# Second modulation in the attention phase: products on GpSimd, sums on ScalarE one unit later, in place of one VectorE instruction

## The chip, the cores and the metric

The kernel runs on one core of a Trainium2 chip. The metric is the device time of one execution in microseconds (us), taken as the median of several runs. The profile is of one execution. Its engines are PE (TensorE: matmuls, with PEld for its weight loads), DVE (VectorE), ACT (ScalarE), POOL (GpSimd) and SP (SyncE, which here only issues DMAs). ACT and POOL issue DMAs as well.

## The reference

One layer of a diffusion backbone: a modulation, differential attention with a residual and a layer norm, a second modulation, and an expert feed-forward with a second residual and layer norm. All data are float32; there are 512 latent tokens, 256 context tokens and a width of 1024.

```python
mod = (s_c @ ada_w[i] + ada_b[i])[:, None, :]          # s_c = silu(c), 1 x 1024; ada_w is 1024 x 6144
sh1, sc1, g1, sh2, sc2, g2 = jnp.split(mod, 6, axis=-1)
u = h * (1.0 + sc1) + sh1
o, oc = diff_attention(uc, u, da_w_in[slot], da_w_out[slot], ...)
h = layer_norm(DN_ALPHA * h + g1 * o, ln_g[i, 0], ln_b[i, 0])
f = peer_ffn(h * (1.0 + sc2) + sh2, peer_wq[i], peer_keys[i], peer_u[i], peer_v[i])
h = layer_norm(DN_ALPHA * h + g2 * f, ln_g[i, 1], ln_b[i, 1])
```

The attention has 8 heads, each with two score maps: `a = softmax(q1 k1) - lam * softmax(q2 k2)`, then `a @ v`, an RMS norm for each head and the output projection. This case is about `g1`, `sh2` and `sc2`: 3 x 1024 numbers, each a dot product of `silu(c)` with one column of `ada_w`.

## The kernel before

The kernel has three phases: attention, mix (rest of the output projection, layer norm, second modulation) and the expert stage (`peer`). Matmuls that need float32 accuracy are made of three matmuls: an operand is split into a rounded high part and a low part, and `mm3` (lines 150, 152 and 153) sums high x high, high x low and low x high. A split is an ACT copy (high, line 142) and a DVE subtraction (low, line 143); `hi_lo` is the helper. Where a helper pins the order, the line is 100.

The modulation that attention itself needs (`sh1`, `sc1`) is computed at the very start with matmuls. The second one, 24 blocks of 128 outputs, runs beside the attention of the heads. Block n is loaded as a tile `adw` with 128 outputs on the partitions and 1024 inputs along the row (512 KB; two buffers). One instruction multiplies it with `sbc`, which is silu(c) repeated on all partitions, and sums each row into column n of `modc`. The function is `ada_units`; each block is a unit. After the last one, `gate` adds the bias, spreads `g1` over a row by transposes on PE, and prepares the columns that mix uses.

For a head, q, k and v are projected (`qkv` banks in PSUM), q and k are rotated (ACT copies `sw`, line 404; DVE products and sums, lines 405, 406 and 424 or 449), split into `kh` (line 142 or 450 on ACT, 143 or 451 on DVE) and sent by DMA from SP into stacked tiles `ks` (line 440) and `qs` (line 456). `kh` has one buffer. Scores (line 523) go to one PSUM tile `sc`; DVE takes row maxima (line 530), ACT the exponentials with row sums (line 534), DVE combines the two maps (line 544, `e`), PE transposes (line 552, `ta`), ACT and DVE split the transposed tile (`at`), and PE multiplies with `vt`. The next score tile can be written only when the exponentials of the one before are done. Weights of the projections come as `wraw` tiles by DMAs from the queue of ACT (line 208), and are split into `whi` and `wlo`.

Three streams of units are merged by due times, which are written by hand in heads: the projections, the attention of the heads, and the second modulation (from 0.55 to 7.9 heads). What is written in that order then goes through a scheduler. It orders each engine's instructions by its own estimate of when each can start, so the order on every engine of the attention phase depends on every unit in it. An instruction on an engine starts in that fixed order; one that has to wait holds back all that stand behind it on the engine, its DMA issues too. The orders of mix and the expert stage are pinned, or come out the same in both kernels.

Of the kernel before, what the change touches and what calls it, by code (L numbers as in the profile page):

```python
# [15 lines left out]
AF = mybir.ActivationFunctionType  # L16
OP = mybir.AluOpType
# [88 lines left out]
class Net:  # L106
# [75 lines left out]
    def attention(self):  # L182
        nc, a, tc = self.nc, self.a, self.tc
        self.dram = self.es.enter_context(tc.tile_pool(name="dram", bufs=1, space=bass.MemoryType.DRAM))
        self.sd = self.dram.tile([1, D], F32, name="sd")
        op = self.onpool = tc.alloc_tile_pool(name="on", bufs=1, side="right")

        one = lambda x: op.tile([128, T], x, name="osc", bufs=H + 1)
# [34 lines left out]
        with tc.tile_pool(name="st", bufs=1) as st, tc.tile_pool(name="stp", bufs=1, space=PSUM) as sp:  # L223
# [20 lines left out]
            AW, MP, HL = {}, {}, {}  # L244
# [113 lines left out]
        sbc = ap.tile([128, D], F32, name="sbc")  # L358
# [261 lines left out]
            return [(h + 1 + lag - (LAST if h == 7 else 0) + 0.25 * x, (0, e, p, 1)) for x, e, p in sorted(out, key=lambda u: u[0])]  # L620

        def ada_units(n0, n1):
            def one(n):
                def go():
                    for k in (n, n + 1):
                        if k < n1 and k not in AW:
                            AW[k] = ap.tile([128, D], F32, name="adw", bufs=2)
                            nc.scalar.dma_start(AW[k], a["ada_b2"][k])
                    ins = nc.vector.scalar_tensor_tensor(AW[n], AW[n], 1.0, sbc, op0=OP.mult, op1=OP.mult,
                                                         accum_out=self.modc[:, n:n + 1])  # L630
                    if self.mark:
                        self.behind(ins, self.mark)
                return (1000, None, go)
            return [one(n) for n in range(n0, n1)]

        AW, self.WH, Z = {}, {}, {}
        self.mark = None
# [67 lines left out]
        for h in range(H):  # L705
            if h < 6:
                A += timed(qkv_units(h), h)
            B += attn_units(h)
        G += timed(ada_units(0, 24), ADA_FROM, GATES_AT - ADA_FROM)
        G.append((GATES_AT, (0, gate, None)))  # L710
        A += timed(qkv_units(6) + qkv_units(7), 6, 1.5)
# [757 lines left out]
```

## Time and profile before

| | us |
|---|---|
| median of 3 runs | 1654.32 |
| the three runs | 1653.97, 1654.32, 1658.24 |
| the profiled execution, its own time | 1652.39 |
| its span (first to last instruction) | 1650.5 |

The profile's idle time names what ended the wait ("<-DMA qs<-kh": the load of `qs` landed last). "PEclk" is the granted clock of TensorE as a share of full speed. Matmuls are pipelined: their durations overlap, so the starts tell the rate.

### The profile page before, as it was taken

The numbers are of one execution on the slowest core, as the hardware profiler recorded it, in microseconds if no ns is written. First come the engines' busy times: TensorE is split into PE (matmuls) and PEld (weight loads), VectorE is DVE, ScalarE is ACT, GpSimd is POOL, SyncE is SP. The second block draws the span as 40 slices with busy tenths as digits, with TensorE's granted clock in tenths as the row PEclk, the third lists the DMA queues.
The fourth block names the chain that finished last, engine by engine and source line by source line (L and its number), as shares of the span: only waits on it lengthen the run. The fifth ranks groups of instructions, "written<-read, shape, count | busy, mean of one in ns | idle before, by whom it ended". The sixth has DMA issues, their size and how long they took to land.

```text
span 1650.5 us, 24717 instructions
## 1 busy us (share of the span) xinstructions
PE 1602.9 (97%) x9229; PEld 1435.6 (87%) x9229; DVE 1422.3 (86%) x2515; ACT 771.8 (47%) x1161; POOL 637.6 (39%) x367
## 2 busy tenths in 40 slices
PE   8899999998999999999999999999999999999997
PEld 5789898986889999999999997888888888888885
DVE  6688888797799999989999848998998989999887
ACT  7565666554433344565566643332333333333332
POOL 0000000000176676535533316665656656655421
PEclk9999999999999999999999999999999999999998
DMA  8644546513432566898899999999999999999982
GB/s 334 182 142 122 156 121 162 168 52 131 156 140 100 159 207 196 283 339 276 301 339 351 347 380 365 358 375 370 386 386 385 388 378 391 390 370 347 341 298 86
DMA packets 134346, 443.80 MB, mean 269 GB/s; under 512 B 13137, under 2 KB 39249, under 8 KB 122962
## 3 DMA queue, kind: packets, MB, share of 16 engines
q1 hardware_dynamic: 79506, 210.88, 37.3%
q0 software_dynamic: 37440, 136.33, 22.1%
q10 hardware_dynamic: 17280, 95.01, 15.6%
q8 instruction: 72, 1.18, 0.3%
q14 instruction: 48, 0.39, 0.1%
HBM read 376.76 MB, written 50.73 MB: 259 GB/s over the span
## 4 chain that ended last, share of the span: by engine, by line
PE 77%; DVE 7%; DMA 6%; issue 5%; POOL 2%; ACT 2%; SPq 0%; ACTq 0%; DVEq 0%; POOLq 0%
PE a L150 10%; PE a L153 10%; PE a L152 10%; PE v L153 9%; PE v L150 9%; PE v L152 9%; PE v L100 4%; PE qkv L150 3%; PE qkv L152 3%; PE qkv L153 3%; PE sc L523 3%; DMA gr<-in_peer_u_dram,eidx 2%; POOL gr L1230 1%; POOL ulo L1154 1%; DMA qs<-kh 1%
## 5 line engine op out<-in xcount | busy, mean ns | idle before, releaser
L150 PE MATMUL a<-u2h,uhi 128*128 128x384 f32 x1024 | 345.5, 337 | 0.2 <-ACT at L100 0.2
L153 PE MATMUL a<-u2h,ulo 128*128 128x384 f32 x1024 | 343.6, 336 | 1.4 <-POOL ulo L1154 1.4
L152 PE MATMUL a<-u2l,uhi 128*128 128x384 f32 x1024 | 343.0, 335 | 0.0
L153 PE MATMUL v<-vh,wl 128*128 128x512 f32 x768 | 300.5, 391 | 3.8 <-DVE wl L143 3.8
L150 PE MATMUL v<-vh,wh 128*128 128x512 f32 x768 | 299.6, 390 | 2.9 <-ACT wh L142 1.5
L152 PE MATMUL v<-vl,wh 128*128 128x512 f32 x768 | 300.1, 391 | 0.1
L1230 POOL DMA_INDIRECT gr<-in_peer_u_dram,eidx x128 | 189.7, 1482 | 245.8 <-DVE gr L1239 230.5
L1154 POOL TENSOR_TENSOR ulo<-ur,uhi 128x1024 fp32r<-128x1024 f32 x77 | 207.4, 2699 | 100.6 <-ACT uhi L100 74.2
L1230 POOL DMA_INDIRECT gr<-in_peer_v_dram,eidx x128 | 180.2, 1408 | 147.1 <-DVE facc L1246 132.3
L142 ACT ACTIVATE vh<-vr 128x1024 fp32r<-128x1024 f32 x126 | 132.7, 1055 | 210.8 <-PE v L153 83.7
L100 POOL TENSOR_TENSOR qlo<-qraw,qhi 128x1024 fp32r<-128x1024 f32 x12 | 28.8, 2399 | 457.6 <-DVE val L100 435.5
L150 PEld LDWEIGHTS a<-u2h,uhi 128*128 128x128 f32 x1024 | 192.8, 188 | 1.8 <-ACT at L100 0.5
L153 PEld LDWEIGHTS a<-u2h,ulo 128*128 128x128 f32 x1024 | 192.6, 188 | 1.8 <-POOL ulo L1154 1.7
L152 PEld LDWEIGHTS a<-u2l,uhi 128*128 128x128 f32 x1024 | 192.9, 188 | 1.3
L143 DVE TENSOR_TENSOR vl<-vr,vh 128x1024 fp32r<-128x1024 f32 x126 | 158.7, 1260 | 30.5 <-ACT vh L142 30.3
L153 PEld LDWEIGHTS v<-vh,wl 128*128 128x128 f32 x768 | 144.5, 188 | 35.7 <-DVE wl L143 5.5
L150 PEld LDWEIGHTS v<-vh,wh 128*128 128x128 f32 x768 | 144.6, 188 | 33.2 <-ACT wh L142 2.2
L1246 DVE SCALAR_TENSOR_TENSOR facc<-gr,act,facc 128x1024 f32<-128x1024 f32 x127 | 166.9, 1314 | 4.2 <-DMA gr<-in_peer_v_dram,eidx 4.2
L152 PEld LDWEIGHTS v<-vl,wh 128*128 128x128 f32 x768 | 144.4, 188 | 29.9 <-DVE vl L143 0.5
L100 ACT ACTIVATE at<-a 128x384 f32<-128x384 f32 x98 | 48.3, 493 | 204.3 <-PE a L153 103.9
L142 ACT ACTIVATE wh<-w 128x384 fp32r<-128x384 f32 x126 | 64.9, 519 | 128.1 <-DVE w L1293 67.4
L143 DVE TENSOR_TENSOR wl<-w,wh 128x384 fp32r<-128x384 f32 x126 | 87.6, 696 | 20.5 <-ACT wh L142 19.4
(281 smaller groups left out, 3258.3 us busy)
## 6 DMA issues: line engine op xcount, KB each, us to landing
ur<-in_u_t_dram SPq DMA_DIRECT2D x128, 512.0 KB, 6.0
vr<-in_v_t_dram ACTq DMA_DIRECT2D x64, 1024.0 KB, 8.6
gq<-gd SPq DMA_DIRECT2D x16, 1536.0 KB, 12.2
gd<-w SPq DMA_DIRECT2D x12, 1920.0 KB, 8.2
ad<-at SPq DMA_DIRECT2D x49, 384.0 KB, 5.8
ar<-ad SPq DMA_DIRECT2D x49, 384.0 KB, 7.2
adw<-in_ada_b_dram ACTq DMA_DIRECT2D x24, 512.0 KB, 3.8
wraw<-in_w_qkv_dram ACTq DMA_DIRECT2D x21, 512.0 KB, 4.4
```

Source lines behind the costliest of these rows:

```text
L100: ins = getattr(self.engine, name)(*args, **kwargs)
L142: (hi_engine or nc.scalar).activation(hi, src, AF.Copy)
L143: return (lo_engine or nc.vector).tensor_tensor(lo, src, hi.bitcast(F32), op=OP.subtract)
L150: ins = nc.tensor.matmul(out, lh, rh, start=first and i == 0, stop=False)
L152: nc.tensor.matmul(out, lh, rl, start=False, stop=False)
L153: ins = nc.tensor.matmul(out, ll, rh, start=False, stop=last and i == n - 1)
L523: nc.tensor.matmul(ps[:, c, n0:n1], QS[h, c][:, v, t * 128:(t + 1) * 128], KS[h, c][:, n0:n1], start=v == 0, stop=v == 1)
L1154: self.paced = (lo_engine or self.nc.gpsimd).tensor_tensor(lo, raw, hi.bitcast(F32), op=OP.subtract)
L1230: ins = nc.gpsimd.indirect_dma_start(out=self.GR[n], out_offset=None, in_=a["peer_v"] if n >= K else a["peer_u"], in_offset=bass.IndirectO ...
L1246: ins = nc.vector.scalar_tensor_tensor(self.facc, r, self.act[:, k:k + 1], self.facc, op0=OP.mult, op1=OP.add)
```

## The change

The multiply-and-sum on DVE is gone. Unit n now does three things: ACT sums the product of block n-1 (a copy in place with an accumulated row sum into `modc`), ACT issues the loads that are due, and GpSimd multiplies block n with `sbc` in place. There are 25 units in place of 24 in the same stretch of due times; the last one only sums. The tie of the DVE instruction to the row maximum before it (`self.mark`) has nothing left to hold.

```diff
         def ada_units(n0, n1):
+
             def one(n):
                 def go():
+                    if n > n0:
+                        nc.scalar.activation(AW[n - 1], AW[n - 1], AF.Copy, accum_out=self.modc[:, n - 1:n])
                     for k in (n, n + 1):
                         if k < n1 and k not in AW:
                             AW[k] = ap.tile([128, D], F32, name="adw", bufs=2)
                             nc.scalar.dma_start(AW[k], a["ada_b2"][k])
-                    ins = nc.vector.scalar_tensor_tensor(AW[n], AW[n], 1.0, sbc, op0=OP.mult, op1=OP.mult,
-                                                         accum_out=self.modc[:, n:n + 1])
-                    if self.mark:
-                        self.behind(ins, self.mark)
+                    if n < n1:
+                        nc.gpsimd.tensor_tensor(AW[n], AW[n], sbc, op=OP.mult)
                 return (1000, None, go)
-            return [one(n) for n in range(n0, n1)]
+            return [one(n) for n in range(n0, n1 + 1)]
```

In the built program POOL has the 24 products in one row ahead of all its other work. The lines of the changed kernel are 627 (the sum), 631 (the load) and 633 (the product); what stands behind line 629 before stands one line lower. The other engines hold the same instructions in another order, in the attention phase alone. Two places:

On ACT, ahead of the first scores of head 0. `kh` of line 450 is the high part of q of head 0, `whi` the first weight split after the start, `wraw` and `adw` are loads. Before:

```order
L142 ACTIVATE vt<-qkv 128x128
L208 DMA wraw<-in_w_qkv_dram 128x1024
L628 DMA adw<-in_ada_b_dram 128x1024
L142 ACTIVATE vt<-qkv 128x256
L142 ACTIVATE vt<-qkv 128x128
L142 ACTIVATE whi<-wraw 128x1024
L450 ACTIVATE kh<-kf 128x512
L208 DMA wraw<-in_w_qkv_dram 128x1024
```

and now:

```order
L142 ACTIVATE vt<-qkv 128x256
L208 DMA wraw<-in_w_qkv_dram 128x1024
L142 ACTIVATE vt<-qkv 128x128
L627 ACTIVATE adw,modc<-adw 128x1024
L450 ACTIVATE kh<-kf 128x512
L142 ACTIVATE whi<-wraw 128x1024
L631 DMA adw<-in_ada_b_dram 128x1024
L142 ACTIVATE vt<-qkv 128x256
L208 DMA wraw<-in_w_qkv_dram 128x1024
```

The high part of q has moved ahead of the weight split, and stands behind the first sum; the following loads of `adw` and `wraw` stand behind it.

On DVE at the same place. Line 451 is the low part of q of head 0, line 530 the first row maximum. Before:

```order
L143 TENSOR_TENSOR wlo<-wraw,whi 128x1024
L451 SCALAR_TENSOR_TENSOR kh<-kf,kh 128x512
L143 TENSOR_TENSOR vt<-qkv,vt 128x256 x2
L143 TENSOR_TENSOR vt<-qkv,vt 128x128
L143 TENSOR_TENSOR wlo<-wraw,whi 128x1024
L143 TENSOR_TENSOR vt<-qkv,vt 128x128
L143 TENSOR_TENSOR wlo<-wraw,whi 128x1024
L530 TENSOR_REDUCE m<-sc 128x2
```

and now:

```order
L451 SCALAR_TENSOR_TENSOR kh<-kf,kh 128x512
L143 TENSOR_TENSOR wlo<-wraw,whi 128x1024
L143 TENSOR_TENSOR vt<-qkv,vt 128x256 x2
L143 TENSOR_TENSOR vt<-qkv,vt 128x128 x2
L530 TENSOR_REDUCE m<-sc 128x2
L143 TENSOR_TENSOR wlo<-wraw,whi 128x1024 x2
```

The low part of q has moved ahead of the first weight split, and the second and third weight splits behind the first row maximum. On PE five matmuls of 512 columns with the first split weights stand ahead of the first scores, where nine stood before; the other four follow behind them.

## Rows read from the trace of the kernel before

**Rows 1.** The page's head, and its first part: busy us of each engine (share of the span) and instructions.

```profile
span 1650.5 us, 24717 instructions
PE 1602.9 (97%) x9229; PEld 1435.6 (87%) x9229; DVE 1422.3 (86%) x2515; ACT 771.8 (47%) x1161; POOL 637.6 (39%) x367
```

**Rows 2.** Busy time by stretches of the attention phase: stretch, its length, busy us (instructions) of PE, PEld, DVE, ACT and POOL, then the granted clock, DMA share and GB/s.

```profile
57.00:80.00 23.00, 17.30 (x131) 16.40 (x131) 13.20 (x25) 10.99 (x20) 0.00 (x0) 0.95 0.83 225
80.00:100.00 20.00, 19.99 (x101) 16.65 (x100) 12.82 (x18) 11.20 (x21) 0.00 (x0) 0.89 0.32 98
100.00:340.00 240.00, 234.52 (x1568) 212.49 (x1567) 202.54 (x395) 148.86 (x301) 0.00 (x0) 1.00 0.52 151
340.00:372.00 32.00, 31.48 (x181) 26.89 (x180) 30.08 (x57) 16.67 (x34) 0.00 (x0) 1.00 0.07 21
```

**Rows 3.** The timeline of PE from 57 to 340 us: start, us, what, and in brackets the idle time ahead of it with what ended it. The five longest waits.

```profile
63.43 0.38 PE L150 MATMUL qkv<-whi,uh 128*128 128x256 f32 x1 [0.57 <-DVE kf L405]
...
79.52 1.62 PE L523 MATMUL sc<-ks,qs 128*128 128x512 f32 x4 [5.13 <-DMA qs<-kh]
...
116.78 0.94 PE L523 MATMUL sc<-ks,qs 128*128 128x512 f32 x4 [1.58 <-DMA ks<-kh]
...
262.33 0.93 PE L523 MATMUL sc<-ks,qs 128*128 128x512 f32 x4 [1.53 <-DMA ks<-kh]
...
322.10 1.67 PE L523 MATMUL sc<-ks,qs 128*128 128x512 f32 x8 [1.15 <-ACT e L534]
```

**Rows 4.** Busy time by stretches around the longest wait (columns as in rows 2).

```profile
74.00:79.50 5.50, 0.39 (x2) 0.01 (x1) 2.28 (x3) 1.06 (x1) 0.00 (x0) 0.83 1.01 248
79.50:84.70 5.20, 5.18 (x14) 4.19 (x15) 0.00 (x0) 0.00 (x0) 0.00 (x0) 0.52 0.73 195
100.00:120.00 20.00, 18.42 (x116) 16.23 (x115) 18.14 (x30) 12.80 (x26) 0.00 (x0) 1.00 0.69 196
```

**Rows 5.** The start of the chain to the first scores, from the timelines of DVE, ACT and SP (columns as in rows 3; SPq and ACTq are DMA issues).

```profile
57.74 1.22 DVE L629 SCALAR_TENSOR_TENSOR adw<-adw,sbc 128x1024 f32<-128x1024 f32 x1
58.88 0.69 DVE L424 TENSOR_TENSOR kf<-kf,sw 128x512 f32<-128x512 f32 x1
...
67.29 1.06 ACT L142 ACTIVATE whi<-wraw 128x1024 fp32r<-128x1024 f32 x1 [1.88 <-DMA wraw<-in_w_qkv_dram]
68.26 0.61 ACT L450 ACTIVATE kh<-kf 128x512 fp32r<-128x512 f32 x1
...
69.53 0.68 DVE L451 SCALAR_TENSOR_TENSOR kh<-kf,kh 128x512 fp32r<-128x512 f32 x1
70.24 3.98 SPq L456 DMA_DIRECT2D qs<-kh  x4
```

**Rows 6.** DMA issues from 64 to 84 us (first three) and from 205 to 225 us (last): out<-in, queue, count, KB each, median us from issue to landing.

```profile
wraw<-in_w_qkv_dram ACTq DMA_DIRECT2D x4, 512.0 KB, 6.5
adw<-in_ada_b_dram ACTq DMA_DIRECT2D x2, 512.0 KB, 6.6
qs<-kh SPq DMA_DIRECT2D x4, 256.0 KB, 8.7
...
qs<-kh SPq DMA_DIRECT2D x4, 256.0 KB, 4.3
```

**Rows 7.** The instructions of the tile `adw`: count, ns of one (min/median/max), first and last start.

```profile
L629 DVE SCALAR_TENSOR_TENSOR adw<-adw,sbc x24: 1206/1216/1221, 57.7 to 330.6; 128x1024 f32<-128x1024 f32 x24
L629 DVE DVE_READ_ACCUMULATOR adw<-adw,sbc x24: 72/82/84, 58.9 to 331.7; 128x1 f32 x24
```

**Rows 8.** Groups of instructions with their shapes: count, busy us, mean ns of one, idle time ahead. The first two are ACT from 80 to 340 us, the third POOL from 435 to 510 us.

```profile
L142 ACT ACTIVATE whi<-wraw 128x1024 fp32r<-128x1024 f32 x20 | 21.2, 1062 | 18.1 <-PE qkv L152 16.3 <-PE qkv L153 1.8
...
L534 ACT ACTIVATION_READ_ACCUMULATOR e<-sc,m 128x1 f32 x56 | 11.1, 198 | 0.0
...
L100 POOL TENSOR_TENSOR qlo<-qraw,qhi 128x1024 fp32r<-128x1024 f32 x12 | 28.8, 2399 | 457.6 <-DVE val L100 435.5 <-ACT qhi L100 18.0 <-DMA ur<-in_u_t_dram 4.1
```

**Rows 9.** The expert stage, timelines: one product row of POOL, and DVE's row beside it; first the same DVE instruction at a time without one.

```profile
1088.15 0.55 DVE L1293 TENSOR_TENSOR w<-gq,ar 128x384 f32<-128x384 f32 x1
...
1376.70 3.01 POOL L1154 TENSOR_TENSOR ulo<-ur,uhi 128x1024 fp32r<-128x1024 f32 x1 [0.60 <-ACT uhi L1153]
...
1377.37 2.76 DVE L1293 TENSOR_TENSOR w<-gq,ar 128x384 f32<-128x384 f32 x1
```

**Rows 10.** The expert stage from 1000 to 1600 us, groups with their shapes (columns as in rows 8).

```profile
L1154 POOL TENSOR_TENSOR ulo<-ur,uhi 128x1024 fp32r<-128x1024 f32 x26 | 70.8, 2722 | 9.3 <-ACT uhi L1153 8.9
...
L143 DVE TENSOR_TENSOR wl<-w,wh 128x384 fp32r<-128x384 f32 x117 | 80.6, 689 | 19.8 <-ACT wh L142 18.8
L1293 DVE TENSOR_TENSOR w<-gq,ar 128x384 f32<-128x384 f32 x88 | 57.9, 676 | 1.1 <-DMA ar<-ad 1.1
L1293 DVE TENSOR_TENSOR w<-gq,at 128x384 f32<-128x384 f32 x29 | 18.1, 623 | 0.0
```

**Rows 11.** DVE from 80 to 340 us, groups with their shapes (columns as in rows 8): the largest whose two inputs both lie in SBUF.

```profile
L544 DVE SCALAR_TENSOR_TENSOR e<-e,m,e 128x768 f32<-128x768 f32 x28 | 28.4, 1015 | 0.4
...
L143 DVE TENSOR_TENSOR wlo<-wraw,whi 128x1024 fp32r<-128x1024 f32 x20 | 24.3, 1217 | 5.3 <-ACT whi L142 5.2
...
L406 DVE TENSOR_TENSOR sw<-sw,sinT 128x512 f32<-128x512 f32 x14 | 9.5, 682 | 0.0
...
L451 DVE SCALAR_TENSOR_TENSOR kh<-kf,kh 128x512 fp32r<-128x512 f32 x7 | 4.8, 687 | 2.5 <-ACT kh L450 2.5
```

## The prediction

> **What bounds the kernel now.** I read the page's first part, then the busy time by stretches, then the waits on PE's timeline. PE is busy 1602.9 of 1650.5 us [rows 1], so time is won only where PE waits or runs at a lower clock. The change touches the attention phase alone. From 57 to 80 us PE is busy 17.30 of 23.0 us, idle 5.7; from 100 to 340 us it is idle 5.5 of 240 [rows 2]. DVE is the next engine there: 202.54 of 240 us, against 148.86 on ACT and nothing on POOL. So DVE is worth relieving only as far as its lateness makes PE wait.
>
> Where PE waits: 5.13 us for `qs` of head 0, 0.57 before that for `kf`, and later 1.58 and 1.53 for `ks` and 1.15 for an exponential [rows 3]. The long wait has a second price. For the next 5.2 us the granted clock is 0.52, the lower level (1.2 of 2.4 GHz), and PE is busy throughout [rows 4]; at full clock that work takes 5.2 x 0.52 = 2.7 us, so 2.5 us are lost. After the wait of 1.58 us at 116.78 the clock stays at 1.00 [rows 3, 4]. Everything to be had in the phase is thus about 5.7 + 2.5 + 5.5 = 13.7 us.
>
> **What is removed and added.** DVE loses 24 instructions of 1.216 us and 24 accumulator reads of 0.082 [rows 7]: 31.1 us. ACT gains 24 copies of 128 x 1024 with a row sum. The same copy without a sum takes 1.06, an accumulator read 0.20 [rows 8]: 1.26 each, 30.2 us, of which some 22/24 fall into the 240 us and take ACT from 62% to 74% busy. POOL gains 24 products of 128 x 1024 at 2.40 each [rows 8], 58 us on an engine that is idle there. The loads are the same 24, now issued behind the sum that frees their buffer instead of waiting for DVE.
>
> POOL's work isn't free for DVE. In the expert stage a DVE product of two SBUF tiles takes 0.55 us alone, and 2.76 when it starts inside a POOL product; the POOL row ends at 1379.7 and it at 1380.1, about its own time later [rows 9]. So a DVE instruction of that kind is held until POOL is done. How often? From 1000 to 1600 us there are 26 POOL products [rows 10]. Against the 0.55 us of a free one, three DVE forms of that size are longer by 117 x 0.139 + 88 x 0.126 + 29 x 0.073 = 29.5 us, or 1.13 per POOL product. The attention phase shows none of this, so the bounds are 0 and a whole product, 2.40. There fewer of DVE's instructions read two SBUF tiles (`e` 28.4, `wlo` 24.3, `sw` 9.5, one of the `kh` 4.8 us, and some small ones, of 260 us [rows 11]), which argues for less; in rows 10 I left out the longer forms, which argues for more. I take 1.13: 24 x 1.13 = 27 us, between 0 and 58. DVE is then given back 27 of the 31 us it loses.
>
> The Trainium skill says this as a rule (SBUF — State Buffer, "Who interferes with whom"): a DVE instruction with two SBUF inputs contends with a GpSimd instruction that reads SBUF, and one with a single SBUF input doesn't. Rows 9 agree with the first half. By the rule the row maxima and the splits from PSUM, which stand between the others here, would not be held.
>
> **The start, head 0.** Before, the high part of q (line 450) stands behind a weight split that waits 1.88 us for its load; it starts at 68.26, the low part at 69.53 and the sends at 70.24 [rows 5]. ACT was free at 67.29 - 1.88 = 65.41. In the new order the first sum stands there instead: 65.41 + 1.26 = 66.67 for the high part, 0.61 more for the low part, which no longer has `wlo` ahead of it, so the sends go at about 68. Two things shift this. Without `adw` ahead of it, line 424 could start 1.14 us earlier [rows 5]; but the first POOL product can start at the same moment, and if it takes the access first, line 424 starts at 57.74 + 2.40, 1.26 later. I take their middle, nothing; the sends go between 67 and 69.5. They then travel before most of the loads that competed: beside four weight loads and two `adw` loads they took 8.7 us, elsewhere 4.3 [rows 6]. Before, they were issued at 70.24 and awaited until 79.52, 9.3 us; with 6 to 9 us they arrive at 74 to 77. PE reaches the scores at 79.52 - 5.13 = 74.4, about 1 earlier now for the four matmuls that moved behind (the first four score matmuls, 1536 columns, took 1.62 us at half clock [rows 3], so 512 columns take some 0.27 at full). The wait of 5.13 becomes 0.5 to 4.5; I take 2.5, a gain of 2.6 (range 0.5 to 4.6). A wait that short may leave the clock alone: 1.5 of the 2.5 us (0 to 2.5). Against it: two weight splits now stand behind the first row maximum on DVE, and a product can hold them; PE needs them soon after the first scores. I put 1.0 (0 to 2.4). Sum: -2.6 - 1.5 + 1.0 = -3.1 us (from +1.9 to -7.1).
>
> **The heads behind it.** DVE is 31 us lighter by count and 27 heavier by holds. The difference matters little: a hold comes where the order didn't reckon with it, and if it meets `e`, `kf`, `kh` or a low part that PE awaits, PE stands. My choice is that one hold in eight reaches PE, with 1.5 us: 3 x 1.5 = 4.5 (0 to 12, one in three). Of the 5.5 us of idle PE, the waits for `ks` and the exponential end chains through DVE, and I let 3.5 go (0 to 5.5). ACT's 28 us lie in its idle quarter; I charge 0.5 for exponentials that stand behind a sum. Sum +1.5 us (-5.5 to +12.5). From mix on the order is the same, and any shift is passed on.
>
> Together -1.6 us: 1652.39 becomes 1650.8. The profiled execution lies 1.9 below the median of the runs, so on the median: 1654.32 - 1.6 = 1652.7.
>
> **The rivals.**
> Rival 1, the first scores arrive in time. The wait of 5.13 goes whole with its 2.5 us of clock and the 0.57 in front, the holds meet nothing that PE awaits: -8.2, 1646. For it: the new order on ACT and DVE puts q first, and PE's later waits are few and short. Against it: the first product stands on the same chain.
> Rival 2, GpSimd holds DVE. The products have no tie to a place in DVE's order: each starts when its load has landed. If one in three holds reaches PE, that is 8 x 1.5 = 12 us, and with a start that gains only 3 the time is 1654.3 + 9 = 1663. It decides from a third of the products on. For it: rows 9 and 10. Against it: most of rows 11 has slack towards PE, since PE waits only 5.5 us there now.
> The page's rule named above is this rival's; the trace agrees so far as rows 9 go.
> Rival 3, the change does nothing. DVE gets its time back in holds, and the start is as late as before since the first sum stands where the load was waited for: 1654.
>
> **How the numbers follow.** 0.3% of this kernel, about 5 us, is what a measurement tells from no change: faster means below 1649.4, slower above 1659.3. My forecast (1648 to 1658) has 0.45, rival 1 0.23, rival 2 0.22, rival 3 0.10. Faster: rival 1 and a little of the forecast, 0.26. Slower: rival 2 but for its mild end, and a little of the forecast's far end, 0.22. Within 0.3%: 0.52. The forecast's own range is 1648 to 1658; with most of rivals 1 and 2 it is 1645 to 1663.
>
> **What would show it.** The start is right if line 450 starts before 67.5 us, `qs` is awaited under 4 us and the clock stays at full after it; wrong if the sends still go after 70. The holds are right if `wlo` (1.22 before), `e` (1.02) and `sw` (0.68) show single rows of 2 to 3.5 us beside POOL, and their means rise by 27 us in sum; wrong if these stay as they are, when DVE should fall by 31 us. ACT should show 24 sums of 1.26 and POOL 24 rows near 2.4. The forecast fails on the fast side if PE's idle time from 57 to 340 us falls under 6 us, on the slow side if it rises over 20.

## The result and the profile after

The changed kernel takes 1666.08 us (median of 4 runs, 1665.21 to 1668.34) against 1654.83 for the kernel before beside it: ratio 1.0067, 95% interval 1.0051 to 1.0083. It is 11 us slower. The forecast was 1652.7, and the time lies outside its range.

The page's head and first part, changed kernel:

```profile
span 1663.4 us, 24751 instructions
...
PE 1602.9 (96%) x9229; PEld 1434.3 (86%) x9229; DVE 1420.0 (85%) x2467; ACT 796.5 (48%) x1209; POOL 698.7 (42%) x391
```

One number hardly moved: DVE has 48 instructions fewer than in [rows 1] and is 2.3 us less busy, though the removed ones were 31 us in sum [rows 7]. Its other instructions became longer. PE is busy for the same 1602.9 us in a span 12.9 longer.

Busy time by stretches, changed kernel (columns as in [rows 2]):

```profile
57.00:80.00 23.00, 16.43 (x120) 15.40 (x119) 9.38 (x17) 11.83 (x24) 6.37 (x3) 0.92 0.73 191
80.00:100.00 20.00, 18.14 (x91) 15.04 (x90) 13.24 (x15) 8.70 (x16) 4.81 (x2) 0.92 0.35 110
100.00:340.00 240.00, 225.76 (x1505) 203.90 (x1504) 188.34 (x338) 164.59 (x332) 49.14 (x19) 0.99 0.51 143
```

PE's idle time from 57 to 340 us is 6.57 + 1.86 + 14.24 = 22.7 us; in [rows 2] it is 5.70 + 0.01 + 5.48 = 11.2. These 11.5 us are the loss, and most of them (8.8) lie behind the start, where only small waits had stood.

The tile `adw`, changed kernel (columns as in [rows 7]). The prices are as worked out: 2.40 us for a product, 1.06 + 0.19 for a sum.

```profile
L633 POOL TENSOR_TENSOR adw<-adw,sbc x24: 2342/2402/3372, 56.2 to 307.3; 128x1024 f32<-128x1024 f32 x24
L627 ACT ACTIVATE adw<-adw x24: 1040/1060/1077, 64.9 to 314.7; 128x1024 f32<-128x1024 f32 x24
L627 ACT ACTIVATION_READ_ACCUMULATOR adw<-adw x24: 182/190/219, 65.9 to 315.7; 128x1 f32 x24
```

The timeline of DVE, changed kernel: all rows from 55 to 345 us that are over 1 us longer than others of their form (start, us, what):

```profile
56.39 2.78 DVE L424 TENSOR_TENSOR kf<-kf,sw 128x512 f32<-128x512 f32 x1
...
94.49 1.76 DVE L542 SCALAR_TENSOR_TENSOR m<-m,nlam,s 128x1 f32<-128x1 f32 x1
...
131.21 2.81 DVE L143 TENSOR_TENSOR wlo<-wraw,whi 128x1024 fp32r<-128x1024 f32 x1
...
142.79 2.89 DVE L451 SCALAR_TENSOR_TENSOR kh<-kf,kh 128x512 fp32r<-128x512 f32 x1
...
163.05 3.10 DVE L143 TENSOR_TENSOR wlo<-wraw,whi 128x1024 fp32r<-128x1024 f32 x1
...
189.36 2.62 DVE L143 TENSOR_TENSOR kh<-kf,kh 128x512 fp32r<-128x512 f32 x1 [1.04 <-ACT kh L142]
...
201.60 2.89 DVE L424 TENSOR_TENSOR kf<-kf,sw 128x512 f32<-128x512 f32 x1
...
208.93 2.71 DVE L143 TENSOR_TENSOR wlo<-wraw,whi 128x1024 fp32r<-128x1024 f32 x1
...
237.48 2.66 DVE L544 SCALAR_TENSOR_TENSOR e<-e,m,e 128x768 f32<-128x768 f32 x1
...
292.43 3.43 DVE L143 TENSOR_TENSOR wlo<-wraw,whi 128x1024 fp32r<-128x1024 f32 x1
```

and POOL's timeline beside the third and the sixth of them:

```profile
130.54 2.39 POOL L633 TENSOR_TENSOR adw<-adw,sbc 128x1024 f32<-128x1024 f32 x1 [9.43 <-DMA adw<-in_ada_b_dram]
...
189.03 2.40 POOL L633 TENSOR_TENSOR adw<-adw,sbc 128x1024 f32<-128x1024 f32 x1 [12.90 <-DMA adw<-in_ada_b_dram]
```

`wlo` starts at 131.21 inside the product that runs to 132.93, and ends at 134.02, about its own 1.2 us after it: held, as in [rows 9]. Each of the ten overlaps a product; together they are 18.8 us over their usual length, and the kernel before has no such row. All have two inputs in SBUF. In the groups by form, 80 to 340 us, changed kernel (columns as in [rows 11]), the forms that read PSUM kept their length:

```profile
L530 DVE TENSOR_REDUCE m<-sc 128x2 f32<-128x1536 f32 x27 | 47.3, 1752 | 29.0 <-PE sc L523 29.0
L143 DVE TENSOR_TENSOR wlo<-wraw,whi 128x1024 fp32r<-128x1024 f32 x21 | 32.7, 1560 | 3.3 <-ACT whi L142 3.3
...
L143 DVE TENSOR_TENSOR at<-ta,at 128x384 fp32r<-128x384 f32 x50 | 27.2, 550 | 2.7 <-ACT at L142 2.6
...
L451 DVE SCALAR_TENSOR_TENSOR kh<-kf,kh 128x512 fp32r<-128x512 f32 x7 | 7.0, 999 | 3.7 <-ACT kh L450 3.7
```

`wlo` rose from 1217 to 1560 ns and line 451 from 687 to 999 [rows 11]; `at` (one input in PSUM) and the row maximum are as short as ever, though from 55 to 345 us nine `at` and five row maxima start inside a product.

Whether the holds matter is read from the chain that ended last (start, us, what), the stretch 57 to 345 us of the changed kernel:

```profile
56.39 2.79 DVE kf L424
...
94.49 1.76 DVE m L542
...
131.29 2.73 DVE wlo L143
...
142.79 2.89 DVE kh L451
...
201.60 2.90 DVE kf L424
...
209.01 2.63 DVE wlo L143
...
292.43 3.43 DVE wlo L143
```

Seven of the ten held rows stand on it, with 2.1 + 1.5 + 1.6 + 2.2 + 2.2 + 1.5 + 2.2 = 13.3 us over their usual lengths, against a loss of 11 to 13. On PE's own timeline the same time appears as waits that [rows 3] does not have:

```profile
63.02 0.39 PE L150 MATMUL qkv<-whi,uh 128*128 128x256 f32 x1 [1.63 <-DVE kf L405]
...
78.03 1.62 PE L523 MATMUL sc<-ks,qs 128*128 128x512 f32 x4 [4.94 <-issue]
...
97.79 0.85 PE L552 MATMUL ta<-ident,e 128*128 128x128 f32 x6 [1.39 <-DVE e L544]
...
134.07 0.38 PE L152 MATMUL qkv<-wlo,uh 128*128 128x256 f32 x1 [1.33 <-DVE wlo L143]
...
193.39 0.52 PE L552 MATMUL ta<-ident,e 128*128 128x128 f32 x3 [2.12 <-DVE e L544]
...
205.93 0.55 PE L552 MATMUL ta<-ident,e 128*128 128x128 f32 x3 [1.16 <-DVE e L544]
```

The wait at 134.07 ends when the held `wlo` ends. The one at 193.39 is for an `e` of ordinary length (it starts at 192.23) that stood behind the `kh` held at 189.36: DVE works in order, so a hold is paid by whatever is queued behind it. The releaser that a wait names need not be the instruction that was held.

Last, the start. SP's sends of `ks` and `qs` of head 0, changed kernel:

```profile
59.86 2.60 SPq L440 DMA_DIRECT2D ks<-kh  x4
69.10 3.84 SPq L456 DMA_DIRECT2D qs<-kh  x4
```

and the high part of q on ACT:

```profile
67.72 0.63 ACT L450 ACTIVATE kh<-kf 128x512 fp32r<-128x512 f32 x1 [1.67 <-DMA ks<-kh]
```

Line 450 now waits until the sends of `ks` have read `kh`, which has one buffer. Before, it started at 68.26 behind the weight split [rows 5], and the sends, issued from 60.26 on, had landed by 66.19. Now they are issued 0.4 us earlier and land at 67.57. The DMA issues from 55 to 64 us, before and then now (out<-in, queue, count, KB each, median us to landing):

```profile
ks<-kh SPq DMA_DIRECT2D x4, 192.0 KB, 3.3
...
ks<-kh SPq DMA_DIRECT2D x4, 192.0 KB, 5.7
```

An `adw` load that was issued at 63.27 before, behind these sends, is now issued at 59.87 beside the first of them. That this load is what slows them is likely but not shown by a run of its own.

### The profile page after: what moved, and what is told of

Read it like the earlier page. It is cut to its first block, busy times and chain, and to the rows that moved or that the text cites. A ratio compares the mean times of both kernels' runs of the same rounds, so it can differ in the third digit from the quotient of the medians.

```text
span 1663.4 us, 24751 instructions
## 1 busy us (share of the span) xinstructions
PE 1602.9 (96%) x9229; PEld 1434.3 (86%) x9229; DVE 1420.0 (85%) x2467; ACT 796.5 (48%) x1209; POOL 698.7 (42%) x391
## 4 chain that ended last, share of the span: by engine, by line
PE 72%; DVE 10%; DMA 7%; issue 5%; ACT 3%; POOL 2%; SPq 0%; ACTq 0%; DVEq 0%; POOLq 0%
PE a L150 10%; PE a L153 10%; PE a L152 10%; PE v L153 9%; PE v L150 9%; PE v L152 9%; PE v L100 4%; DMA gr<-in_peer_u_dram,eidx 2%; PE qkv L153 2%; PE qkv L150 2%; PE qkv L152 2%; PE sc L523 2%; DMA qs<-kh 2%; POOL gr L1231 1%; POOL ulo L1155 1%
## 5 line engine op out<-in xcount | busy, mean ns | idle before, releaser
L1247 DVE SCALAR_TENSOR_TENSOR facc<-gr,act,facc 128x1024 f32<-128x1024 f32 x127 | 164.7, 1297 | 5.9 <-DMA gr<-in_peer_v_dram,eidx 5.7
L633 POOL TENSOR_TENSOR adw<-adw,sbc 128x1024 f32<-128x1024 f32 x24 | 61.1, 2547 | 248.6 <-DMA adw<-in_ada_b_dram 166.6
L1240 DVE SCALAR_TENSOR_TENSOR gr<-gr,u2t 128x1024 f32<-128x1024 f32 x74 | 94.9, 1306 | 12.1 <-DMA gr<-in_peer_u_dram,eidx 12.1
```

The costliest lines, as they stand in the source:

```text
L633: nc.gpsimd.tensor_tensor(AW[n], AW[n], sbc, op=OP.mult)
L1240: ins = nc.vector.scalar_tensor_tensor(r, r, 1.0, self.row2, op0=OP.mult, op1=OP.mult, accum_out=self.act[:, k:k + 1])
L1247: ins = nc.vector.scalar_tensor_tensor(self.facc, r, self.act[:, k:k + 1], self.facc, op0=OP.mult, op1=OP.add)
```

## The experiments

Theory A: a GpSimd product holds every DVE instruction with two inputs in SBUF until it ends, and the holds reach TensorE. Theory B: the sums on ScalarE are what costs. Theory C: the scheduler's new order costs the time, whatever the engines do. Theory D is about the start: TensorE's wait for `qs` comes of the loads of `adw`, and moving these wins time.

**The product made small.** Only the changed kernel's product is altered, so that PE, DVE, ACT and SP keep its order to the instruction.

```diff
-                        nc.gpsimd.tensor_tensor(AW[n], AW[n], sbc, op=OP.mult)
+                        nc.gpsimd.tensor_tensor(AW[n][:, :8], AW[n][:, :8], sbc[:, :8], op=OP.mult)
```

> The changed kernel with the GpSimd product cut to the first 8 of its 1024 columns (the other 1016 columns are left unmultiplied, so the sums hold something else). Every instruction of the other four engines stands in the same order as in the changed kernel, and the 24 sums on ScalarE still run over 1024 columns. Theory A (a long GpSimd product holds VectorE instructions with two inputs in on-chip memory; ten such holds, 18.9 us in all, stand in the trace of the changed kernel): no VectorE instruction is held, TensorE's idle time between 57 and 340 us falls from 22.7 to 11 to 15 us, time 1654 to 1658. Theory B (the 24 sums on ScalarE, some 30 us, are what TensorE waits for): 1664 to 1668, as now. Theory C (the order of the instructions, which the scheduler laid anew, costs the time): 1664 to 1668, as now.

Measured: 1654.84 us, ratio 0.9992 (0.9976 to 1.0007). The loss is gone, with the sums and the order in place: B and C fall as causes of the 11 us. The stretches of this kernel (columns as above):

```profile
57.00:80.00 23.00, 18.38 (x141) 17.58 (x139) 9.59 (x23) 14.41 (x26) 0.61 (x3) 0.94 0.75 210
80.00:100.00 20.00, 19.54 (x99) 16.39 (x99) 12.54 (x16) 9.49 (x18) 0.40 (x2) 0.90 0.33 107
100.00:340.00 240.00, 233.07 (x1552) 210.84 (x1551) 182.31 (x350) 170.15 (x342) 6.58 (x19) 0.99 0.53 151
```

PE's idle time is 4.62 + 0.46 + 6.93 = 12.0 us. This run shows a second thing: DVE is relieved and nothing is held, and the kernel is still no faster than before, with 12.0 us of idle PE against 11.2. What the change wants to win isn't there, as far as this measurement tells.

**The product cut, and the product twice.** The same loop with 2 pieces of 512 columns, 4 of 256 or 16 of 64; and the whole product issued twice. The order on the other four engines again is the changed kernel's.

```diff
-                        nc.gpsimd.tensor_tensor(AW[n], AW[n], sbc, op=OP.mult)
+                        for q in range(4):
+                            c = slice(256 * q, 256 * q + 256)
+                            nc.gpsimd.tensor_tensor(AW[n][:, c], AW[n][:, c], sbc[:, c], op=OP.mult)
```

Four pieces:

> The changed kernel with each GpSimd product cut into four pieces of 256 columns; the same result, the same bytes, and the other four engines' instructions in the same order as in the changed kernel. Theory A: a VectorE instruction can be held by at most one piece, some 0.6 us, instead of by up to 2.2 us, if the access goes to VectorE between two pieces: holds sum to 5 us or less, time 1655 to 1660. If VectorE has to wait for all four pieces, as now. Theories B and C: 1664 to 1668, as now.

Twice:

> The changed kernel with each GpSimd product issued twice in a row (so that the sums hold the product with the square of the scale); the other four engines' instructions stand in the same order as in the changed kernel. Theory A: twice the time in which VectorE can be held, so about twice the loss against the kernel before: 1674 to 1679. Theories B and C: 1664 to 1669, since GpSimd is idle most of the time and the sums have some 7 us to spare.

Two pieces:

> The changed kernel with each GpSimd product in two pieces of 512 columns; the other engines' order is that of the changed kernel. Theory A, by the three points with this order so far (held time and ratio: none, 0.9992; 9.4 us in quarters, 1.0021; 47 us with the product twice, 1.0189): one piece takes about 1.3 us and holds at most that, held time between the 9.4 us of quarters and the 19 us of whole products, ratio 1.003 to 1.0055. If the cut does not matter: 1.0067 as the changed kernel.

Sixteen pieces:

> The changed kernel with each GpSimd product in sixteen pieces of 64 columns, otherwise as with halves and quarters. Theory A, if a held instruction waits only for the piece that is running: pieces of some 0.3 us, held time under 6 us, ratio 0.9995 to 1.002. If every piece takes the access anew from VectorE, so that the many pieces together hold as long as before: 1.002 to 1.006.

Measured. In all six kernels the first 502 instructions of DVE end with the last row maximum of the attention phase (line 530), in the same order. What DVE is busier up to there than in the first row of the table is held time, small holds included. Behind it the six kernels are the same, and DVE's busy time still differs by up to 5.7 us from one profile to the other (1127.4 to 1133.0), so a page's first part can't be used for this. The two stretches for the product of 8 columns and for the change (columns as above, the first up to the end of that row maximum):

```profile
0.00:368.76 368.76, 347.59 (x2258) 302.66 (x2259) 269.15 (x502) 248.23 (x473) 7.80 (x28) 0.98 0.53 161
...
0.00:377.90 377.90, 345.54 (x2258) 301.39 (x2259) 286.93 (x502) 249.21 (x473) 61.33 (x28) 0.99 0.52 157
```

| GpSimd product | ns of a piece | DVE busy to the last row maximum, us | held, us | PE idle, 57 to 340 | ratio (95%) |
|---|---|---|---|---|---|
| 8 columns | 203 | 269.2 | 0 | 12.0 | 0.9992 (0.9976 to 1.0007) |
| 16 x 64 | 324 | 277.1 | 7.9 | 14.0 | 1.0027 (1.0013 to 1.0041) |
| 4 x 256 | 742 | 279.3 | 10.2 | 16.0 | 1.0021 (1.0005 to 1.0037) |
| 2 x 512 | 1297 | 287.2 | 18.1 | 19.8 | 1.0057 (1.0036 to 1.0079) |
| 1 x 1024 (the change) | 2402 | 286.9 | 17.8 | 22.7 | 1.0067 (1.0051 to 1.0083) |
| 2 x (1 x 1024) | 2404 and 2411 | 318.3 | 49.2 | 36.8 | 1.0189 (1.0158 to 1.0220) |

Idle PE grows with held DVE: (22.7 - 12.0) / 17.8 = 0.60 us for each held us in the change, 24.8 / 49.2 = 0.50 for the product twice, 0.43 for two pieces, 0.39 for four and 0.25 for sixteen. So half of a held microsecond or somewhat more reaches TensorE when the holds are long, and less when they are short. That is theory A with a size. A rival that a small product alone leaves open, that the sum on ScalarE and the next load come late because the product takes long, falls here too: sixteen pieces take 16 x 0.324 = 5.2 us for each product instead of 2.4 and lose less, and no instruction of ScalarE waits for a product in the changed kernel.

Cutting makes each hold shorter, but one product can then hold more instructions. The change has 11 rows of DVE over 0.25 us longer than with the small product, 19.2 us in sum; two pieces have 24 such rows, none over 1.2 us longer, and again 19.2; four pieces have 21 with 10.0. Sixteen pieces have only 4, 1.9 us in sum, beside many very small holds. Four pieces and sixteen can't be told apart in time, nor two pieces and the whole product.

The expectations were low for the product twice (1674 to 1679; measured 1690.0), for the holds with four pieces (5 us or less; measured 10.2) and for sixteen pieces (0.9995 to 1.002; measured 1.0027, in the range of their rival); two pieces came just above theirs (1.0055; measured 1.0057). The product twice loses 35.2 us against the small product, more than its 24.8 us of idle PE. The granted clock fell there too, 0.95 in place of 0.99 from 100 to 340 us, which by these rows is an estimated 0.04 x 240 = 10 us:

```profile
100.00:340.00 240.00, 212.60 (x1330) 189.53 (x1331) 199.02 (x297) 151.13 (x301) 98.29 (x39) 0.95 0.47 129
```

**The sums made small.**

```diff
-                        nc.scalar.activation(AW[n - 1], AW[n - 1], AF.Copy, accum_out=self.modc[:, n - 1:n])
+                        nc.scalar.activation(AW[n - 1][:, :8], AW[n - 1][:, :8], AF.Copy, accum_out=self.modc[:, n - 1:n])
```

> The changed kernel with each sum on ScalarE cut to the first 8 of 1024 columns (the rest of the sum is left out); the products stay whole. ScalarE loses some 1 us of 1.25 per unit, 22 us in all; the scheduler lays the order somewhat otherwise (some 480 of 10043 TensorE instructions move). Theory A: still 1662 to 1668. Theory B: 1654 to 1658. Theory C: any of 1650 to 1670, since the order is another.

Measured: 1662.44 us, ratio 1.0033 (1.0015 to 1.0051). Half of the loss or so remains without ScalarE's work, at A's lower end. DVE is busy 284.5 us up to the last row maximum here, 15.3 held, which by the table stands for 1.002 to 1.007. The order is another, so this run alone would not decide.

**The products on VectorE**, sums on ScalarE.

```diff
-                        nc.gpsimd.tensor_tensor(AW[n], AW[n], sbc, op=OP.mult)
+                        nc.vector.tensor_tensor(AW[n], AW[n], sbc, op=OP.mult)
```

> The changed kernel with the products back on VectorE (without their sums) and the sums left on ScalarE, so that GpSimd does nothing here. The scheduler lays another order (some 932 of 10043 TensorE instructions stand elsewhere than in the kernel before). Theory A (GpSimd's holds are the loss): no VectorE instruction is held, ratio to the kernel before 0.998 to 1.002. Theory B (the sums on ScalarE are part of the loss): 1.003 to 1.007, with TensorE waiting for ScalarE after sums.

Measured: 1657.67 us, ratio 1.0010 (0.9993 to 1.0027). As A expects: in a third order, with ScalarE's sums and no product on GpSimd, nothing measurable is lost. That is a second blow to B, though the interval leaves room for 4 us, and PE is idle for 15.0 us from 57 to 340 us in the profiled execution, against 11.2 before.

**GpSimd work beside the kernel before.** DVE's multiply-and-sum stays; behind it GpSimd multiplies the same two tiles, or fills the tile with zeros twice. Nobody reads either.

```diff
                     if self.mark:
                         self.behind(ins, self.mark)
+                    nc.gpsimd.tensor_tensor(AW[n], AW[n], sbc, op=OP.mult)
```

> The kernel before, with its VectorE instruction for product and sum kept, and one more product of GpSimd over the same two tiles behind it (a result that nobody reads; ScalarE has no sums). The scheduler moves some 318 of 10043 TensorE instructions. Theory A: the holds alone make the loss, without the sums on ScalarE and without the changed kernel's order: by the ratio of the runs so far (about two thirds of the held time reach the end, 0.8 us held for each product) 24 x 0.8 x 0.65 = 12 us, and some more since VectorE has 31 us more of two-input work to be held: 1667 to 1675 against 1655 to 1657. If the holds are harmful only together with the sums on ScalarE or that order: 1653 to 1660.

```diff
                     if self.mark:
                         self.behind(ins, self.mark)
+                    nc.gpsimd.memset(AW[n], 0.0)
+                    nc.gpsimd.memset(AW[n], 0.0)
```

> The same place as in the run with the product beside it, but GpSimd only fills the tile with zeros, twice (no input is read; a result that nobody reads). It asks what it is in GpSimd's work that holds VectorE. If it is GpSimd's reading of two inputs: no VectorE instruction is longer than in the kernel before, 1653 to 1659. If any work of GpSimd in on-chip memory holds VectorE: holds as with the product in proportion to the time of the fills, 1660 to 1672.

Measured: product 1683.01 us, ratio 1.0155 (1.0124 to 1.0187); fill 1664.89, ratio 1.0042 (1.0021 to 1.0063). The product is more harmful here than in the change, and than A expected (1667 to 1675): DVE is busy 333.8 us up to the last row maximum, 40.9 more than in the kernel before (292.9), since most products start right when DVE's own `adw` ends and meet what comes next. Groups on DVE from 80 to 340 us with the product beside (columns as above):

```profile
L143 DVE TENSOR_TENSOR wlo<-wraw,whi 128x1024 fp32r<-128x1024 f32 x18 | 32.1, 1782 | 1.1 <-ACT whi L142 1.1
...
L542 DVE SCALAR_TENSOR_TENSOR m<-m,nlam,s 128x1 f32<-128x1 f32 x25 | 17.5, 698 | 0.3
```

and with the fill:

```profile
L143 DVE TENSOR_TENSOR wlo<-wraw,whi 128x1024 fp32r<-128x1024 f32 x20 | 24.3, 1214 | 2.2 <-ACT whi L142 2.1
...
L597 DVE TENSOR_SCALAR v<-v 128x4 int32<-128x4 int32 x6 | 4.6, 772 | 0.1
```

The fill leaves `wlo` at 1214 ns, though seven of them start inside a fill: it is GpSimd's reading that holds a two-input instruction. The Trainium skill says so (SBUF — State Buffer, "Who interferes with whom"): two SBUF inputs contend with a GpSimd instruction that reads SBUF, not with one that only writes it; the trace agrees, 1782 against 1214 ns. But the fill's time isn't that of the kernel before: 1.0042, in the range that was expected if any work of GpSimd holds VectorE. DVE is busy 296.3 us up to the last row maximum, 3.4 more than before, about what `v` of line 597 takes more (4.6 against 1.0 us). No long wait of PE ends at `v`; the longest later one is 4.26 us for `ks` at 269.49, where the kernel before waits 1.53 [rows 3]. The scheduler moved some 311 of TensorE's instructions, and the fills keep the buffers longer; which of these makes the 7 us stays open, and so part of the product's 1.0155 may not be holds.

**The start, with later due times.** The units are due from 1.15 (or 0.95) of a head on.

```diff
-ADA_FROM = 0.55
+ADA_FROM = 1.15
```

The changed kernel with four pieces:

> The changed kernel in quarters with the units of the second modulation due from 1.15 of a head on instead of 0.55, so that the scheduler puts two fewer of its loads ahead of the first sends of q, and the rounding of q ahead of the first weights. Theory D (at the start TensorE waits some 5 us for the sends of q, and these are late because they share the DMA engines with those loads): the wait falls from 5 to 2 to 3 us, 1652 to 1657, and the time is 2 to 4 us under that of the quarters alone. Its rival (the sends are late because of the weights' loads or because the buffer of k has to be sent first): 1657 to 1661, as the quarters alone.

The kernel before, 1.15:

> The kernel before with the same later due time, product and sum on VectorE as they were. Theory D: 1649 to 1653, that is 2 to 5 us under the kernel before, with the wait for q at the start at 2 to 3 us instead of 5.13. Its rival: within 2 us of the kernel before.

The kernel before, 0.95:

> The kernel before with the units of the second modulation due from 0.95 of a head on (1.15 in the earlier run, which stood at 0.9984). It asks whether a kernel faster than both comes of theory D. If the wait for the sends of q at the start is what a later due time wins: 0.996 to 0.999, with that wait at 2 to 3 us. If what is won there is lost again behind, at the waits for the sends of k: 0.999 to 1.002.

Measured: 1659.97, 1653.93 and 1655.01 us, ratios 1.0025 (1.0009 to 1.0040), 0.9984 (0.9966 to 1.0002) and 1.0000 (0.9986 to 1.0015). The wait that D speaks of does shrink (to 1.90, 2.28 and 0.79 us), and no gain clear of the noise follows; the second one's interval leaves room for 5 us. The third kernel shows both. Its stretches (columns as above):

```profile
57.00:80.00 23.00, 21.64 (x152) 19.95 (x151) 13.08 (x23) 10.95 (x21) 0.00 (x0) 1.00 0.84 241
80.00:100.00 20.00, 20.00 (x119) 17.17 (x118) 18.46 (x28) 15.54 (x31) 0.00 (x0) 1.00 0.34 101
100.00:340.00 240.00, 229.50 (x1518) 206.96 (x1517) 195.57 (x382) 143.04 (x290) 0.00 (x0) 0.99 0.51 147
```

and three of PE's waits:

```profile
77.63 0.94 PE L523 MATMUL sc<-ks,qs 128*128 128x256 f32 x4 [0.79 <-issue]
...
111.88 0.94 PE L523 MATMUL sc<-ks,qs 128*128 128x512 f32 x4 [1.42 <-DMA ks<-kh]
...
184.79 1.25 PE L523 MATMUL sc<-ks,qs 128*128 128x512 f32 x4 [2.16 <-DMA ks<-kh]
```

The wait of 5.13 us at the start [rows 3] is down to 0.79, the clock stands at 1.00 in both first stretches, and idle PE from 57 to 100 us falls from 5.7 to 1.4. From 100 to 340 us it rises from 5.5 to 10.5, mostly in waits ahead of the scores of later heads: 11.9 in all against 11.2. The four pieces with a later due time do the same (1.9 + 0.0 + 14.9 = 16.8 against 16.0). Why the later heads give it back isn't settled; no version here is faster than the kernel before by more than the measurement can tell.

## Why the prediction was wrong

**What held.** The prices (2.40, 1.06 + 0.19), the kind of instruction that is held and, within its wide range, the held sum: 27 us were expected within 0 to 58, 17.8 measured. The sign that was named for the slow side, more than 20 us of idle PE, came: 22.7.

**The step that failed: "one hold in eight reaches PE, with 1.5 us: 3 x 1.5 = 4.5".** Of 24 products ten held an instruction by over 1 us, and seven of these are on the chain, 1.9 us each: 13.3 us. By the kernels of one order half of the held time or somewhat more reaches TensorE when whole products hold (0.50 and 0.60), not 4.5 of 27, a sixth. The reason given was that most of the two-input forms have slack towards PE because PE waits little. The chain shows otherwise: it runs through lines 424 and 451, `wlo` and the small `m`, which end the chains that bring k, q and weights to TensorE, and DVE's order passes a hold on to `e`. So few waits of PE did not mean that DVE's instructions had slack. This is rival 2, nearly to its number: 8 x 1.5 = 12 us of holds, 1663 with a gain of 3 at the start that did not come, and 1666 without it.

**"I let 3.5 go" of the later idle time.** With no holds and DVE relieved (the small product) nothing went: 12.0 us idle against 11.2, ratio 0.9992. DVE's load was no bound. (The lower end of that paragraph's sum is -5.0, not -5.5, with its own 0.5 for ScalarE.)

**The start, "-2.6 - 1.5 + 1.0".** None of its three signs came: line 450 at 67.72 instead of before 67.5, a wait of 4.94 instead of under 4, and no full clock after it (0.51 in the 5.2 us from 78.0 to 83.2). The wait gained 0.2, the clock nothing, and of the 1.0 put down for the weight splits a wait of 0.46 us for `wlo` at 87.50 is seen. The working took ACT to be free for q at 65.41 and the high part to start at 66.67. ACT was free at 66.05, but the working left out that `kh` has one buffer: line 450 waits for the sends of `ks`, and these land 1.4 us later than before, though issued 0.4 earlier. In the kernel with units due from 0.95 of a head on, where the next `adw` load is issued at 62.61, behind the sends, they take 3.2 us again and line 450 starts at 66.01. The first product also took the access just ahead of line 424 (56.20 against 56.39), the bad side of the two that were averaged; line 424 still ends at 59.17, 0.4 us earlier than before, so this did not make the start late. And the later due times suggest that a mended start would have been given back behind it.

**Sizes.** The 24 instructions of 1.216 + 0.082 are 31.1 us in sum, but only 25.7 us of DVE's time in the trace of the kernel before is theirs alone: neighbours on DVE overlap by some 0.1 us at each end [rows 5], so summed durations overstate what leaves.

## What to carry to other kernels

Before moving elementwise work from VectorE to GpSimd, list VectorE's instructions with two SBUF inputs and see how many stand on the chain that ended last: each can be held for a whole GpSimd instruction, and here 0.5 to 0.6 of that time reached TensorE. Relieving an engine that is 84% busy was worth nothing measurable here, since TensorE's waits end at chains (sends, single buffers) that don't get shorter. If the work must go to GpSimd, cut it finely enough: four pieces held 10.2 instead of 17.8 us at the price of 4 x 0.742 - 2.402 = 0.57 us more per product on an idle engine; two pieces held as much as the whole, and sixteen were no better in time than four.

## What the runs showed of the hardware

- A small instruction is held as long as a big one: `m` of 128 x 1, usually 0.22 us, took 1.76 at 94.49 in the changed kernel, 1.5 us more; `wlo` of 128 x 1024 took 1.5 to 2.2 us more.
- A GpSimd product costs (2402 - 1297) / 512 = 2.16 ns per column and some 0.19 us per instruction, which also gives 742 and 324 ns for 256 and 64 columns.
- One form with a single SBUF input is held too: `v` of lines 596 and 597, one input and constants, 4 columns of int32. Line 597 takes 772 ns beside the fill against 171 with the small product; with two pieces three rows of line 596 take 0.58, 1.26 and 1.26 us beside a product. The group of line 597 with the small product:

```profile
L597 DVE TENSOR_SCALAR v<-v 128x4 int32<-128x4 int32 x6 | 1.0, 171 | 0.2
```

The Trainium skill (SBUF — State Buffer, "Who interferes with whom") names this form as one that can run in a mode with both ports and then contends with GpSimd, without the condition that the latter reads; the trace agrees for line 597, 0.6 us at a time. The prediction gave the rule for a single SBUF input without this exception.
